# First layer's opening in a two-layer decoder trunk: row tiles abreast, norm weights and identity made on GpSimd, 13 unread products on TensorE

## The chip, the cores and the metric

One core of a Trainium2 chip runs the whole program. The metric is the device time of one execution in microseconds (us); lower is better. TensorE is PE in the profile (PEld its weight loads), VectorE is DVE, ScalarE is ACT, GpSimd is POOL, SyncE is SP. SP issues nearly all DMAs.

## The reference, cut to what matters

Two layers, each on 256 rows of 1024 (two row tiles of 128 rows), float32. The opening of a layer is a norm and an input projection; the rest of a layer (gated recurrence, compressed, selected and window attention, output projection, SwiGLU) is not touched.

```
for l in range(DEPTH):
    xn = rms_norm(h, norm_mix[l])            # x * rsqrt(mean(x*x) + 1e-6) * gain
    proj = xn @ w_in[l]                      # 1024 x 3352
    (hq, hf, hi, hg, nq, kc, vc, ksl, vsl, ksw, vsw, ngate) = split(proj)
    ...
    kc = compress(kc, pe_k, w1_k, w2_k); vc = compress(vc, pe_v, w1_v, w2_v)
    h = h + mix @ w_out[l]; h = h + ffn(rms_norm(h, norm_ffn[l]))
```

## The kernel before, in words

Every float32 product is made of three products of split halves: each weight tile (a "unit", up to 128x1024 float32) is loaded by SP into one of four buffers `wraw`, ACT copies it to a rounded high part `whi` (L142), DVE subtracts to a low part `wlo` (L143), and `mm3` (L319) issues high x high, low x high, high x low on PE. A raw buffer comes free when DVE has made `wlo`; there are six pairs of `whi`/`wlo`. `weights(i)` (L146) asks for splits AHEAD = 5 units ahead and loads NRAW = 4 further.

Units of a layer come in the order B (four units of 128x1024, the columns of kc, vc, ksl, vsl), C (four of 128x560: ksw, vsw, gates), A (four of 128x1024: the queries), then the recurrence's. I call them W0 to W3 (B), W4 to W7 (C), W8 to W11 (A).

The opening of layer 0: `norm_T` (L324) takes one row tile: ACT squares both halves with a row sum (L332), POOL makes the factor `n_ss` (L334, L335), DVE multiplies by factor and gain into `xn` (L338), PE transposes (`pxn`, L341), ACT copies the high part of the turned tile (L346), DVE subtracts the low part (L347). It is called for row tile 0 and then for row tile 1. The gain of the norm stands in one row; PE spreads it over 128 partitions with two products into PSUM (`pgain`, L249). The identity for transposes is loaded with the constants (L209). `setup_late` (L276) and `setup_tables` (L294) then make small vectors on DVE and rotary tables on POOL.

After B's products (`pt`, L322) ACT copies the first 256 columns of a row tile into `kvc` (L439), and PE transposes `kvc` into `pa` (L453). The compression's weights `w1` (L465: eight DMAs of 512 KB, k and v in turn, four steps) are multiplied in `phid` (L505) after A.

A scheduler of the framework puts the instructions of each engine into one fixed order before the run; each engine's sequencer, SP's too, works through its own row in order, and a wait holds up all that stands behind it. DMAs carry one of eight semaphores in turn; a DMA is issued only when the one eight before it has landed.

Of the kernel before, what the change touches and what calls it, by code (L numbers as in the profile page):

```python
# [23 lines left out]
EPS = 1e-6  # L24
# [65 lines left out]
def trunk(ctx: ExitStack, tc: tile.TileContext, x, w_in, w_out, lbl, gnorm, q_gain, k_gain,  # L90
          pe_k, w1_k, w2_k, pe_v, w1_v, w2_v, w_ffi, w_ffo, norm_mix, norm_ffn, consts, out):
    nc = tc.nc
# [11 lines left out]
    def bank(name, tag):  # L104
        return ps.tile([128, 512], F32, name=name, tag=tag, bufs=BANKS[tag])


    units = []

    def unit(src, a, b):  # L110
        units.append([src, a, b, None, None, None, None])
        return len(units) - 1

    state = {"loaded": 0, "split": 0}
# [11 lines left out]
    def after(ins, others):  # L126
        for o in others:
            tc.add_manual_dep(ins.ins, o.ins.name,
                              mybir.DependencyInfo(mybir.DependencyClass.NoSync, mybir.DependencyReason.DATA),
                              reason="fewer table loads")  # L130

    def split_to(n):
        while state["split"] < min(n, len(units)):
            load_to(state["split"] + 1)
            u = units[state["split"]]
            a, b = u[1], u[2]
            hi = wsp.tile([128, 1024], F32R, name="whi")
            lo = wsp.tile([128, 1024], F32R, name="wlo")
            u[4] = hi[:, : a * b].rearrange("p (a b) -> p a b", b=b)
            u[5] = lo[:, : a * b].rearrange("p (a b) -> p a b", b=b)  # L140
            with tc.high_priority(offset=SPLIT_PRIO):
                after(S.activation(u[4], u[3], AF.Copy), state.pop("behind", ()))  # L142
# [65 lines left out]
    cst = one.tile([128, NKEEP], F32, name="cst")  # L208
# [21 lines left out]
    def C(name, parts=128):  # L230
        lo, hi = _L[name]
        return cst[:parts, lo:hi]

    ident = C("ident")
    cos = C("cos").rearrange("p (t d) -> p t d", d=64)
    sin = C("sin").rearrange("p (t d) -> p t d", d=64)

# [6 lines left out]
    ones = one.tile([128, 128], F32, name="ones")
    nc.gpsimd.memset(ones[0:1], 1.0)
    gain0 = []
    for a in range(2):
# [6 lines left out]
    tabc = one.tile([128, NL, 2, 64], F32, name="tabc")  # L254

    kB = one.tile([128, 2, 2, T], F32R, name="kB")
    for g in range(2):
        nc.gpsimd.memset(kB[64 - 64 * g:128 - 64 * g, g].bitcast(F32), 0.0)

    def rstd(ss, n, div, name, scr=None):  # L260

# [14 lines left out]
    def setup_late():  # L276
        p = bank("prow", "c")
        PE.transpose(p[:, :NROW], rows[:NROW, :], ident[:NROW, :NROW])
        V.tensor_copy(vecs, p[:, :NROW])
        z = vecs[:, 0:8].rearrange("p (l h) -> p l h", h=4)  # L280
        mx = sm.tile([128, 4], F32, name="lbm")
        e = sm.tile([128, NL, 4], F32, name="lbe")
        sx = sm.tile([128, 4], F32, name="lbs")
        V.tensor_max(mx, z[:, 0], z[:, 1])
        V.tensor_sub(e, z, mx[:, None, :].to_broadcast([128, NL, 4]))
        S.activation(e, e, AF.Exp)
        V.tensor_add(sx, e[:, 0], e[:, 1])
        V.reciprocal(sx, sx)
        V.tensor_mul(e, e, sx[:, None, :].to_broadcast([128, NL, 4]))
        V.tensor_add(e[:, 1], e[:, 0], e[:, 1])  # L290
        V.tensor_sub(lb, e, e[:, 0:1].to_broadcast([128, NL, 4]))
        V.tensor_scalar(omlb, lb, -1.0, 1.0, op0=OP.mult, op1=OP.add)

    def setup_tables():  # L294
        G = nc.gpsimd
        V.tensor_copy(idb, ident)
        V.tensor_copy(cab, tmp0[:, :128])
        V.tensor_copy(lev_m, tmp0[:, 128:448])
        for l in range(NL):
            gq = qk_g[:, 64 * l:64 * l + 64]  # L300
            ks = [qk_g[:, NL * 64 + 192 * l + 64 * b:NL * 64 + 192 * l + 64 * b + 64] for b in range(3)]
            for i, g in enumerate((gq, ks[1], ks[2])):
                gb = g[:, None, :].to_broadcast([128, NT, 64])
                G.tensor_mul(tabs[:, l, i, 0], cos, gb)
                for a in range(2):
                    s0, s1 = slice(32 * a, 32 * a + 32), slice(32 - 32 * a, 64 - 32 * a)
                    G.tensor_mul(tabs[:, l, i, 1, :, s0], sin[:, :, s0],
                                 g[:, None, s1].to_broadcast([128, NT, 32]))
                if i == 0:
                    G.tensor_scalar(tabs[:, l, i], tabs[:, l, i], 0.125, None, op0=OP.mult)  # L310
            G.tensor_mul(tabc[:32, l, 0], C("cosc", 32), ks[0][:32])
            for a in range(2):
                s0, s1 = slice(32 * a, 32 * a + 32), slice(32 - 32 * a, 64 - 32 * a)
                G.tensor_mul(tabc[:32, l, 1, s0], C("sinc", 32)[:, s0], ks[0][:32, s1])


    products = []
# [6 lines left out]
    def norm_T(t, gain, xh, xl, tag, behind=(), hold=None):  # L324

        with tc.high_priority():
            ss = sm.tile([128, 4], F32, name="n_ss")
            lo = []
            xn = wk.tile([128, D], F32, name="xn", tag="vs", bufs=2)
            for a in range(2):  # L330
                cs = slice(512 * a, 512 * a + 512)
                sq = S.activation(xn[:, cs], h[:, t, cs], AF.Square, scale=D ** -0.5, accum_out=ss[:, a:a + 1])  # L332
                after(sq, behind)
# [22 lines left out]
    for l in range(NL):  # L356
        U = UN[l]
        gain1 = load_gain(norm_ffn[l])
        X = xT()
        last = [norm_T(0, gain0, *X[:2], "c", hold=end + HOLD[0] if l else None)[0]]  # L360
# [63 lines left out]
        def rope_k(src, b, t):  # L424
# [464 lines left out]
        X = X2  # L889
# [129 lines left out]
```

## Time and profile before

| | |
|---|---|
| median of 3 runs | 692.9 us (692.88 to 694.86) |
| the profiled execution's own time | 694.62 us |
| its span, first to last instruction | 692.2 us |
| PE busy | 674.9 us, 98% of the span |
| DVE, ACT, POOL busy | 477.8, 379.9, 23.1 us |
| DMA moved | 118.92 MB, mean 172 GB/s |

Time not in the span (694.62 - 692.2 = 2.4 us) lies around it. All starts are us from the span's start. A busy PE includes modelled ends of products, so starts are compared here, not lengths.

### The profile page before, as it was taken

What the parts mean: (1) busy time and instruction counts of PE and PEld (TensorE: products, weight loads), DVE (VectorE), ACT (ScalarE), POOL (GpSimd) and SP (SyncE); (2) the same over time, 40 slices, a digit from 0 to 9 for tenths busy, and PEclk for the clock granted to TensorE, in tenths of its full rate; (3) what the DMA queues carried; (4) which work ended last, traced back from release to release, by engine and by line L of the source; (5) the groups of instructions that cost most, each with busy time, mean ns of one, the idle gap of its engine ahead of it and who ended that gap; (6) DMA issues with size and microseconds to landing.
All of it is one profiled execution on the core that took longest, in us unless ns stands there. A gap on an engine that the chain in (4) does not pass through costs nothing.

```text
span 692.2 us, 10682 instructions
## 1 busy us (share of the span) xinstructions
PE 674.9 (98%) x4031; PEld 567.5 (82%) x4031; DVE 477.8 (69%) x853; ACT 379.9 (55%) x676; POOL 23.1 (3%) x54
## 2 busy tenths in 40 slices
PE   5999999999999999999999999999999999999997
PEld 3869886688988888888878898768898888888886
DVE  4879997586765566665678979958676655666552
ACT  5446766665555555555456557747545555555540
POOL 1700000001000000000010000000000000000000
PEclk9999999999999999999999999999999999999999
DMA  7798521253865566656678632404366665665521
GB/s 242 237 346 261 171 64 59 91 165 105 266 196 183 182 189 195 194 184 190 180 237 293 203 119 63 122 1 124 122 199 204 195 194 186 188 197 191 183 90 61
DMA packets 86568, 118.92 MB, mean 172 GB/s; under 512 B 5035, under 2 KB 69365, under 8 KB 86518
## 3 DMA queue, kind: packets, MB, share of 16 engines
q1 hardware_dynamic: 86518, 118.26, 55.2%
q8 instruction: 31, 0.51, 0.3%
q14 instruction: 19, 0.16, 0.1%
HBM read 117.19 MB, written 1.05 MB: 171 GB/s over the span
## 4 chain that ended last, share of the span: by engine, by line
PE 82%; DVE 7%; DMA 4%; ACT 4%; issue 2%; POOL 1%; SPq 0%; POOLq 0%; DVEq 0%; ACTq 0%
PE pgu L905 20%; PE pz L322 17%; PE pt L322 12%; PE pgu L908 10%; PE py L322 6%; DVE wlo L143 3%; DMA wraw<-in_w_in_dram 3%; PE pl L766 2%; PE pO L667 2%; ACT whi L142 2%; PE pPT L657 2%; PE pf L322 1%; PE pxn L341 1%; DMA wraw<-in_w_ffn_in_dram 1%; PE pq L322 1%
## 5 line engine op out<-in xcount | busy, mean ns | idle before, releaser
L143 DVE TENSOR_TENSOR wlo<-wraw,whi 128x1024 fp32r<-128x1024 f32 (+1 forms) x204 | 245.3, 1206 | 146.9 <-ACT whi L142 145.8
L142 ACT ACTIVATE whi<-wraw 128x1024 fp32r<-128x1024 f32 (+1 forms) x204 | 212.2, 1043 | 154.7 <-PE pgu L905 42.5
L905 PE MATMUL pgu<-x,whi 128*128 128x512 f32 x640 | 174.8, 394 | 0.1
L905 PEld LDWEIGHTS pgu<-x,whi 128*128 128x128 f32 x640 | 110.6, 189 | 16.0 <-DVE ahl L946 0.3
L322 PE MATMUL pz<-whi,ahl 128*128 128x512 f32 x352 | 112.5, 391 | 0.0
L908 PEld LDWEIGHTS pgu<-x,wlo 128*128 128x128 f32 x640 | 98.1, 189 | 13.5
L908 PE MATMUL pgu<-x,wlo 128*128 128x256 f32 x640 | 101.7, 281 | 0.0
L322 PE MATMUL pt<-whi,x 128*128 128x512 f32 (+1 forms) x320 | 100.0, 386 | 0.0
L322 PEld LDWEIGHTS pz<-whi,ahl 128*128 128x128 f32 x352 | 65.9, 188 | 13.9 <-DVE ahl L922 0.5
L322 PE MATMUL pz<-wlo,ahl 128*128 128x512 f32 x176 | 68.9, 392 | 0.0
L322 PEld LDWEIGHTS pt<-whi,x 128*128 128x128 f32 x320 | 57.5, 190 | 8.3 <-DVE x L347 0.5
L322 PE MATMUL pt<-wlo,x 128*128 128x512 f32 (+1 forms) x160 | 62.0, 388 | 0.6 <-DVE wlo L143 0.6
L322 PE MATMUL py<-whi,x 128*128 128x512 f32 x128 | 41.8, 397 | 0.0
L322 PEld LDWEIGHTS pz<-wlo,ahl 128*128 128x128 f32 x176 | 33.0, 188 | 6.4
L322 PEld LDWEIGHTS pt<-wlo,x 128*128 128x128 f32 x160 | 30.5, 191 | 5.3 <-DVE wlo L143 1.5
L587 ACT ACTIVATE P<-pS,nm 128x128 f32<-128x128 f32 (+1 forms) x64 | 26.0, 426 | 6.7 <-DVE nm L634 5.4
L322 PEld LDWEIGHTS py<-whi,x 128*128 128x128 f32 x128 | 24.1, 188 | 4.8
L914 ACT ACTIVATE sl<-sl 128x512 f32<-128x512 f32 x20 | 12.7, 633 | 27.3 <-DVE sl L913 27.3
L766 PEld LDWEIGHTS pl<-Q,K 128*128 128x128 f32 x160 | 23.7, 191 | 3.3 <-issue 0.8
L322 PE MATMUL py<-wlo,x 128*128 128x512 f32 x64 | 25.0, 390 | 0.0
L322 PE MATMUL pf<-x,whi 128*128 128x256 f32 x128 | 23.8, 286 | 0.0
L322 PE MATMUL pgt<-whi,x 128*128 128x256 f32 x128 | 23.8, 285 | 0.0
(220 smaller groups left out, 862.4 us busy)
## 6 DMA issues: line engine op xcount, KB each, us to landing
wraw<-in_w_ffn_in_dram SPq DMA_DIRECT2D x88, 512.0 KB, 3.6
wraw<-in_w_in_dram SPq DMA_DIRECT2D x48, 512.0 KB, 5.0
wraw<-in_w_ffn_out_dram SPq DMA_DIRECT2D x44, 512.0 KB, 3.5
w<-in_cmp_w_k_dram SPq DMA_DIRECT2D x8, 512.0 KB, 5.1
w<-in_cmp_w_v_dram SPq DMA_DIRECT2D x8, 512.0 KB, 7.3
wraw<-in_w_out_dram SPq DMA_DIRECT2D x16, 256.0 KB, 4.0
wraw<-in_w_out_dram SPq DMA_DIRECT2D x8, 512.0 KB, 3.9
wraw<-in_w_in_dram SPq DMA_DIRECT2D x8, 280.0 KB, 5.4
```

The lines of the kernel that those rows point to most:

```text
L142: after(S.activation(u[4], u[3], AF.Copy), state.pop("behind", ()))
L143: u[6] = V.tensor_sub(u[5], u[3], u[4].bitcast(F32))
L322: products.append(PE.matmul(o, a[u], b[v], start=start and i == 0, stop=stop and i == 2, skip_group_check=skip))
L341: tr = PE.transpose(p[:, 128 * k:128 * k + 128], xn[:, 512 * c + 128 * k:512 * c + 128 * k + 128], ident)
L587: e = S.activation(o, i, f, **kw)
L657: PE.transpose(p[:, 128 * hg:128 * hg + 128], P[t, g][:, hg, b, 128 * sb:128 * sb + 128], ident)
L667: m = PE.matmul(po[64 * g:64 * g + 64], vtok[:, b, sb, 64 * g:64 * g + 64], pts[g][0], start=(b == 0 and sb == 0), stop=False, skip_group_ ...
L766: m = PE.matmul(p[:, t0 + 64 * i:t0 + 64 * i + 64], K[:, i, ts], QF[:, i, ts].rearrange("p (n c a) -> p n c a", c=2, a=half)[:, :, 1], sta ...
L905: products.append(PE.matmul(pp[b], w[0][:, k, s], X[2][:, 4 * hh + k].rearrange("p c t -> p (c t)"), start=(hh == 0 and k == 0), stop=Fals ...
L908: products.append(PE.matmul(pp[b][:, T:], w[1][:, k, s], X[0][:, 4 * hh + k], start=False, stop=(hh == 1 and k == 3), skip_group_check=True))
L914: S.activation(sl, sl, AF.Silu)
```

## The change

It writes layer 0's opening as a routine of its own and moves small work about:

- `first_rows` replaces the two calls of `norm_T` in layer 0. It chains the instructions of ACT, DVE and POOL in a written order (tile 0's two halves, W0's split, tile 0's first half turned, tile 1's first half, W1's split, ...); the second halves are turned from inside the loop over B (`second`). `proj_first` walks B as (unit, row tile) = (0,0) (1,0) (0,1) (1,1) (2,0) (2,1) (3,0) (3,1) instead of all units of tile 0 and then of tile 1.
- POOL writes the identity (memset, affine_select) and spreads the gain row (two partition_broadcast of 512); the two products and the identity's DMA are gone. The gain row's DMA is issued by ACT.
- 13 products of a constant bfloat16 tile (128x512) into a bank that nobody reads stand first on PE.
- The zeroing of `kB` and the rotary tables are chained behind the factors on POOL, key tables ahead of query tables. `setup_late` moves behind B. Three casts (idb, cab, lev_m) move behind the split of W11.

```diff
-    DMA.dma_start(grow[0:1], norm_mix[0:1])
+    cst = one.tile([128, NKEEP], F32, name="cst")
+    S.dma_start(grow[0:1], norm_mix[0:1])
...
-    DMA.dma_start(cst[:, :128], consts[:, :128])
...
+    ident = one.tile([128, 128], F32, name="ident")
+    G.memset(ident, 1.0)
+    G.affine_select(ident, ident, pattern=[[-1, 128]], compare_op=OP.is_equal, fill=0.0, base=0, channel_multiplier=1)
+    grows = wk.tile([128, 2, 512], F32, name="grows", tag="P", bufs=1)
...
+        last_pool = G.partition_broadcast(grows[:, a], grow[0:1, 512 * a:512 * a + 512], channels=128)
...
-        gain0.append(bank("pgain", "b"))
-        PE.matmul(gain0[a], ones[0:1], grow[0:1, 512 * a:512 * a + 512], start=True, stop=True)
+    V.memset(idle, 1.0)
+    spin_bank = bank("pspin", "e")
+    def spin(n):
+        for _ in range(n):
+            PE.matmul(spin_bank, idle[:, :128], idle, start=True, stop=True)
+    spin(SPIN)
...
+        with tc.high_priority():
+            squares(0)
+            normed(0, 0)
+            normed(0, 1)
+            split()
+            pv = turned(0, 0)
+            hi(0, 0, pv)
+            lo(0, 0, pv)
+            squares(1)
+            normed(1, 0)
+            split()
+            pv = turned(1, 0)
+            hi(1, 0, pv)
+            lo(1, 0, pv)
+            normed(1, 1)
+        def second(t):
+            with tc.high_priority():
+                pv = turned(t, 1, products[-1:])
+                hi(t, 1, pv)
+                lo(t, 1, pv)
+                split()
...
-        if l == 0:
-            norm_T(1, gain0, *X[:2], "c", last)
-            setup_late()
+        if l:
+            norm_T(0, gain0, *X[:2], "c", hold=end + HOLD[0])
+        else:
+            second = first_rows(*X[:2])
             setup_tables()
...
+        def proj_first(name):
+            ps_ = [bank("pt", "a") for _ in range(NT)]
+            for q, t in ((0, 0), (1, 0), (0, 1), (1, 1), (2, 0), (2, 1), (3, 0), (3, 1)):
+                    w = weights(U[name, q]) if q > 1 and t == 0 else units[U[name, q]][4:6]
...
+                    if (q, t) in ((1, 0), (0, 1)):
+                        second(t)
...
+        if l == 0:
+            setup_late()
```

What the scheduler makes of it, at three places. First SP's DMA issues after the small constants; `gain` is the next norm's weights, `wraw` with 128x2x280 are C's units W4 to W7, `w_...<-in_cmp_w` with 128x4x256 are `w1`. Before:

```order
L200 DMA gain<-in_norm_ffn_dram 128x1024
L122 DMA wraw<-in_w_in_dram 128x2x280 x4
L465 DMA w_355<-in_cmp_w_k_dram 128x4x256
L122 DMA wraw<-in_w_in_dram 128x2x512 x4
L465 DMA w_355<-in_cmp_w_v_dram 128x4x256
L465 DMA w_358<-in_cmp_w_k_dram 128x4x256
```

The same place with the change, with what each issue waits for (a DMA semaphore, and POOL or DVE):

```order
L202 DMA gain<-in_norm_ffn_dram 128x1024 [waits DMAHW4_49,Pool_49]
L566 DMA w_367<-in_cmp_w_k_dram 128x4x256 [waits DMAHW5_49]
L566 DMA w_367<-in_cmp_w_v_dram 128x4x256 [waits DMAHW6_49]
L566 DMA w_370<-in_cmp_w_k_dram 128x4x256 [waits DMAHW7_49]
L566 DMA w_370<-in_cmp_w_v_dram 128x4x256 [waits DMAHW0_49]
L566 DMA w_373<-in_cmp_w_k_dram 128x4x256 [waits DMAHW1_49]
L123 DMA wraw<-in_w_in_dram 128x2x280 [waits DMAHW2_49,DVE_49]
L566 DMA w_373<-in_cmp_w_v_dram 128x4x256 [waits DMAHW3_49]
L566 DMA w_376<-in_cmp_w_k_dram 128x4x256 [waits DMAHW4_49]
L123 DMA wraw<-in_w_in_dram 128x2x280 [waits DMAHW5_49,DVE_49]
L566 DMA w_376<-in_cmp_w_v_dram 128x4x256 [waits DMAHW6_49]
L123 DMA wraw<-in_w_in_dram 128x2x280 [waits DMAHW7_49,DVE_49]
```

The fourth C unit is the next row after these. All eight `w1` loads now stand ahead of W7, five of them ahead of W4; before, the four C units stood ahead of all of them.

Second ACT's row around the end of B; 128x1024 and 128x560 `whi` are splits of B's and C's units. Before:

```order
L346 ACTIVATE x_128<-pxn 128x4x128 x2
L439 ACTIVATE kvc<-pt 128x512
L420 ACTIVATE sqk<-pt 128x128
L442 ACTIVATE vtok<-pt 128x128
L286 ACTIVATE lbe<-lbe 128x8
L142 ACTIVATE whi<-wraw 128x560 x3
L439 ACTIVATE kvc<-pt 128x512
L142 ACTIVATE whi<-wraw 128x560
```

With the change:

```order
L366 ACTIVATE x_141<-pxn 128x4x128
L143 ACTIVATE whi<-wraw 128x1024
L143 ACTIVATE whi<-wraw 128x560 x4
L538 ACTIVATE kvc<-pt 128x512
L505 ACTIVATE sqk<-pt 128x128
L541 ACTIVATE vtok<-pt 128x128
L538 ACTIVATE kvc<-pt 128x512
```

Both copies to `kvc` now stand behind the splits of all four C units, W7's among them; before, the first stood ahead of all of them and the second ahead of W7's.

Third PE's row from B's end on. Before (two rows of B's last products, then the rest):

```order
L322 MATMUL pt<-wlo,x_128 128x512
L322 MATMUL pt<-whi,x_128 128x512
L453 MATMUL pa<-cst,kvc 128x128 x2
L322 MATMUL pt<-whi,x_128 128x280
L322 MATMUL pt<-wlo,x_128 128x280
```

With the change, with waits:

```order
L528 MATMUL pt<-wlo,x_141 128x512 x2
L289 MATMUL prow<-ident,tmp_92 128x74 [waits DMAHW4_49,DMAHW3_49,DMAHW5_49,DMAHW2_49,PE_49]
L554 MATMUL pa<-ident,kvc 128x128 [waits Activation_49]
L554 MATMUL pa<-ident,kvc 128x128 [waits PE_49]
L335 MATMUL pt<-whi,x_141 128x280
L335 MATMUL pt<-wlo,x_141 128x280 [waits DVE_49]
```

In both, the first transposes of `kvc` stand ahead of C's first product.

## Rows read from the trace of the kernel before

**Rows 1.** The page: busy time of PE, its busy tenths in 40 slices.

```profile
PE 674.9 (98%) x4031; PEld 567.5 (82%) x4031; DVE 477.8 (69%) x853; ACT 379.9 (55%) x676; POOL 23.1 (3%) x54
...
PE   5999999999999999999999999999999999999997
```

**Rows 2.** Timeline of PE, opening (start us, us, what, count, idle before and its releaser).

```profile
11.83 1.97 PE L341 MATMUL pxn<-cst,xn 128*128 128x128 f32 x8 [5.78 <-DVE xn L338]
...
14.65 1.05 PE L322 MATMUL pt<-whi,x 128*128 128x512 f32 x2
15.51 0.53 PE L322 MATMUL pt<-wlo,x 128*128 128x512 f32 x1
15.88 0.63 PE L322 MATMUL pt<-whi,x 128*128 128x512 f32 x2
16.34 0.40 PE L322 MATMUL pt<-wlo,x 128*128 128x512 f32 x1
...
20.21 0.63 PE L341 MATMUL pxn<-cst,xn 128*128 128x128 f32 x4
...
27.16 0.38 PE L453 MATMUL pa<-cst,kvc 128*128 128x128 f32 x2
```

**Rows 3.** Timeline of ACT: the split of W0.

```profile
8.80 1.06 ACT L142 ACTIVATE whi<-wraw 128x1024 fp32r<-128x1024 f32 x1 [3.48 <-DMA wraw<-in_w_in_dram]
```

**Rows 4.** Timeline of POOL: the last memset, then the factor of row tile 0.

```profile
2.04 0.14 POOL L548 MEMSET kcz<- 128x64 f32 x1
...
5.42 0.29 POOL L334 TENSOR_SCALAR n_ss<-n_ss 128x1 f32<-128x1 f32 x1 [3.24 <-ACT xn L332]
5.80 0.57 POOL L335 TENSOR_TENSOR n_ss<-n_ss,mhalf 128x1 f32<-128x1 f32 x1
```

**Rows 5.** Timeline of DVE: normed halves, a unit's low part, a turned half's low part.

```profile
11.03 1.40 DVE L338 SCALAR_TENSOR_TENSOR xn<-h,n_ss,pgain 128x512 f32<-128x512 f32 x2
...
12.52 1.22 DVE L143 TENSOR_TENSOR wlo<-wraw,whi 128x1024 fp32r<-128x1024 f32 x1
...
13.66 0.68 DVE L347 TENSOR_TENSOR x<-pxn,x 128x512 fp32r<-128x512 f32 x1
```

**Rows 6.** Timeline of SP's queue: first issues, and those from the next norm's gain on.

```profile
0.72 0.36 SPq L205 DMA_DIRECT2D gain<-in_norm_mix_dram  x1
...
2.00 0.43 SPq L209 DMA_DIRECT2D cst<-in_consts_dram  x1
...
16.80 0.39 SPq L200 DMA_DIRECT2D gain<-in_norm_ffn_dram  x1
...
17.30 1.92 SPq L122 DMA_DIRECT2D wraw<-in_w_in_dram  x4
...
19.26 0.64 SPq L465 DMA_DIRECT2D w<-in_cmp_w_k_dram  x1
```

**Rows 7.** DMA issues in 16 to 50 us: KB each, median us to landing.

```profile
w<-in_cmp_w_k_dram SPq DMA_DIRECT2D x4, 512.0 KB, 8.0
...
wraw<-in_w_in_dram SPq DMA_DIRECT2D x4, 280.0 KB, 5.4
gain<-in_norm_ffn_dram SPq DMA_DIRECT2D x1, 512.0 KB, 4.7
```

**Rows 8.** Windows: busy us (count) of PE, PEld, DVE, ACT, POOL; clock, DMA share, GB/s.

```profile
21.00:25.00 4.00, 4.00 (x19) 3.30 (x18) 3.87 (x13) 3.30 (x8) 4.00 (x13) 1.00 1.06 354
26.00:29.00 3.00, 2.69 (x17) 2.21 (x16) 2.93 (x6) 1.49 (x4) 3.00 (x8) 1.00 0.02 3
...
40.00:50.00 10.00, 10.00 (x94) 7.18 (x93) 6.78 (x21) 2.03 (x3) 0.00 (x0) 1.00 1.10 348
```

**Rows 9.** Timeline of ACT around B's end: a copy to kvc, a split of 560.

```profile
27.36 0.60 ACT L439 ACTIVATE kvc<-pt 128x512 f32<-128x512 f32 x1 [2.57 <-PE pt L322]
27.86 0.66 ACT L142 ACTIVATE whi<-wraw 128x560 fp32r<-128x560 f32 x1
```

**Rows 10.** Waits of PE's weight loads in 26 to 90 us: total, times, longest.

```profile
PEld pt L322 <- DVE wlo L143: 1.5, 3, 0.8
```

More of the change, by code (lines that the diff above doesn't have):

```diff
@@ L43 @@
 LEV_PRIO, PACE = 250, (0, 7, 2)
+SPIN = 13
 HOLD, HOLD_C = (18, 18, 16, 36), 1
@@ L110, in unit @@
     def unit(src, a, b):
-        units.append([src, a, b, None, None, None, None])
+        units.append([src, a, b] + [None] * 5)
         return len(units) - 1
@@ L141, in split_to @@
             with tc.high_priority(offset=SPLIT_PRIO):
-                after(S.activation(u[4], u[3], AF.Copy), state.pop("behind", ()))
+                u[7] = S.activation(u[4], u[3], AF.Copy)
+                after(u[7], state.pop("behind", ()))
                 u[6] = V.tensor_sub(u[5], u[3], u[4].bitcast(F32))
@@ L232, in C @@
         return cst[:parts, lo:hi]
-    ident = C("ident")
+    G = nc.gpsimd
+    ident = one.tile([128, 128], F32, name="ident")
+    G.memset(ident, 1.0)
+    G.affine_select(ident, ident, pattern=[[-1, 128]], compare_op=OP.is_equal, fill=0.0, base=0, channel_multiplier=1)
+    grows = wk.tile([128, 2, 512], F32, name="grows", tag="P", bufs=1)
+    gain0 = []
+    for a in range(2):
+        last_pool = G.partition_broadcast(grows[:, a], grow[0:1, 512 * a:512 * a + 512], channels=128)
+        gain0.append(grows[:, a])
     cos = C("cos").rearrange("p (t d) -> p t d", d=64)
@@ L243, in trunk @@
     nc.gpsimd.memset(mhalf, -0.5)
[L244 to L247, printed above, removed]
-        gain0.append(bank("pgain", "b"))
-        PE.matmul(gain0[a], ones[0:1], grow[0:1, 512 * a:512 * a + 512], start=True, stop=True)
+    idle = one.tile([128, 512], BF16, name="idle")
+    V.memset(idle, 1.0)
[4 more added lines that the diff above has]
+    spin(SPIN)
     vecs = one.tile([128, NROW], F32, name="vecs")
@@ L256, in trunk @@
     kB = one.tile([128, 2, 2, T], F32R, name="kB")
-    for g in range(2):
-        nc.gpsimd.memset(kB[64 - 64 * g:128 - 64 * g, g].bitcast(F32), 0.0)
     def rstd(ss, n, div, name, scr=None):
@@ L294, in setup_tables, with then @@
     def setup_tables():
[L295 to L298, printed above, removed]
+        def then(ins):
+            after(ins, pool_order[-1:])
+            pool_order.append(ins)
+        for g in range(2):
+            then(G.memset(kB[64 - 64 * g:128 - 64 * g, g].bitcast(F32), 0.0))
         for l in range(NL):
@@ L301, in setup_tables @@
             ks = [qk_g[:, NL * 64 + 192 * l + 64 * b:NL * 64 + 192 * l + 64 * b + 64] for b in range(3)]
[L302 removed]
+            for i, g in ((1, ks[1]), (2, ks[2]), (0, gq)):
                 gb = g[:, None, :].to_broadcast([128, NT, 64])
[L304 removed]
+                then(G.tensor_mul(tabs[:, l, i, 0], cos, gb))
                 for a in range(2):
                     s0, s1 = slice(32 * a, 32 * a + 32), slice(32 - 32 * a, 64 - 32 * a)
[L307 to L308 removed]
+                    then(G.tensor_mul(tabs[:, l, i, 1, :, s0], sin[:, :, s0],
+                                      g[:, None, s1].to_broadcast([128, NT, 32])))
                 if i == 0:
[L310 to L311 removed]
+                    then(G.tensor_scalar(tabs[:, l, i], tabs[:, l, i], 0.125, None, op0=OP.mult))
+            then(G.tensor_mul(tabc[:32, l, 0], C("cosc", 32), ks[0][:32]))
             for a in range(2):
                 s0, s1 = slice(32 * a, 32 * a + 32), slice(32 - 32 * a, 64 - 32 * a)
[L314 removed]
+                then(G.tensor_mul(tabc[:32, l, 1, s0], C("sinc", 32)[:, s0], ks[0][:32, s1]))
     products = []
@@ L322, in mm3, with first_rows, then, split @@
             products.append(PE.matmul(o, a[u], b[v], start=start and i == 0, stop=stop and i == 2, skip_group_check=skip))
-    def norm_T(t, gain, xh, xl, tag, behind=(), hold=None):
+    pool_order = []
+    def first_rows(xh, xl):
+        xn, rs, order = [], [], {V: [], S: [], G: [last_pool]}
+        def then(eng, ins):
+            after(ins, order[eng][-1:])
+            order[eng].append(ins)
+        def split():
+            i = state["split"]
+            split_to(i + 1)
+            then(S, units[i][7])
+            then(V, units[i][6])
+        def normed(t, c):
+            cs = slice(512 * c, 512 * c + 512)
+            then(V, V.scalar_tensor_tensor(xn[t][:, cs], h[:, t, cs], rs[t], gain0[c], op0=OP.mult, op1=OP.mult))
+        def turned(t, c, behind=()):
+            p = bank("pxn", "c")
+            for k in range(4):
+                cs = slice(512 * c + 128 * k, 512 * c + 128 * k + 128)
+                after(PE.transpose(p[:, 128 * k:128 * k + 128], xn[t][:, cs], ident), behind)
+            return p.rearrange("p (k t) -> p k t", t=128)
+        def hi(t, c, pv):
+            dh = xh[:, 4 * c:4 * c + 4, 128 * t:128 * t + 128]
+            then(S, S.activation(dh, pv, AF.Copy))
+        def lo(t, c, pv):
+            sl = slice(4 * c, 4 * c + 4), slice(128 * t, 128 * t + 128)
+            then(V, V.tensor_sub(xl[:, sl[0], sl[1]], pv, xh[:, sl[0], sl[1]].bitcast(F32)))
+        def squares(t):
+            ss = sm.tile([128, 4], F32, name="n_ss")
+            xn.append(wk.tile([128, D], F32, name="xn", tag="vs", bufs=2))
+            for a in range(2):
+                cs = slice(512 * a, 512 * a + 512)
+                then(S, S.activation(xn[t][:, cs], h[:, t, cs], AF.Square, scale=D ** -0.5,
+                                     accum_out=ss[:, a:a + 1]))
+            then(G, G.tensor_scalar(ss[:, 2:3], ss[:, 0:1], ss[:, 1:2], EPS, op0=OP.add, op1=OP.add))
+            then(G, G.tensor_tensor(ss[:, 3:4], ss[:, 2:3], mhalf, op=OP.pow))
+            rs.append(ss[:, 3:4])
+        with tc.high_priority():
[19 more added lines that the diff above has]
+                split()
+        pool_order.extend(order[G])
+        return second
@@ L326, in norm_T @@
+    def norm_T(t, gain, xh, xl, tag, hold=None):
         with tc.high_priority():
@@ L331, in norm_T @@
                 cs = slice(512 * a, 512 * a + 512)
-                sq = S.activation(xn[:, cs], h[:, t, cs], AF.Square, scale=D ** -0.5, accum_out=ss[:, a:a + 1])
-                after(sq, behind)
+                S.activation(xn[:, cs], h[:, t, cs], AF.Square, scale=D ** -0.5, accum_out=ss[:, a:a + 1])
             nc.gpsimd.tensor_scalar(ss[:, 2:3], ss[:, 0:1], ss[:, 1:2], EPS, op0=OP.add, op1=OP.add)
@@ L433, in rope_k @@
             V.tensor_add(dst, dst, tmpk)
+        def proj_first(name):
+            ps_ = [bank("pt", "a") for _ in range(NT)]
+            for q, t in ((0, 0), (1, 0), (0, 1), (1, 1), (2, 0), (2, 1), (3, 0), (3, 1)):
+                    w = weights(U[name, q]) if q > 1 and t == 0 else units[U[name, q]][4:6]
+                    ts = slice(128 * t, 128 * t + 128)
+                    for i, (u, v) in enumerate(((0, 0), (1 - q % 2, q % 2), (q % 2, 1 - q % 2))):
+                        for k in range(2):
+                            products.append(PE.matmul(ps_[t], X[v][:, 2 * q + k, ts], w[u][:, k],
+                                                      start=(q + i + k == 0), stop=(q == 3 and i == 2 and k == 1)))
+                    if (q, t) in ((1, 0), (0, 1)):
+                        second(t)
+            return enumerate(ps_)
         begin = len(products)
-        for t, p in proj_tok("B"):
+        for t, p in proj_tok("B") if l else proj_first("B"):
             if l and t == 0:
@@ L494, in trunk @@
         gates(0)
+        if l == 0:
+            for o, i in ((idb, ident), (cab, tmp0[:, :128]), (lev_m, tmp0[:, 128:448])):
+                after(V.tensor_copy(o, i), [units[U["A", 3]][6]])
         p = bank("phid", "e")[:, :256]
```

2 lines of the change are left out of this document (removed).

## The prediction

> **What bounds the kernel now.** I read the page first: PE is busy for 674.9 us of the 692.2 us span, and its busy tenths are 9 in every slice but the first and the last [rows 1]. So the time is PE's work plus PE's holes, and PE's work does not change here (the 13 unread products run while PE has nothing else). Next I read PE's timeline. The first transposes start at 11.83, after an idle stretch of 5.78 us that DVE's `xn` ended; the first transposes of `kvc` (`pa`), which mark B's end, start at 27.16 [rows 2]. Up to there PE loses an opening; after it there are only small holes: its weight loads wait 1.5 us in all for `wlo` in `pt`, in three waits [rows 10]. Last I read what feeds PE after the opening. Products of B take 0.23 us from start to start, so PE eats a unit of 512 KB in 12 products, 2.8 us; the DMA engines are full wherever SP has issued (354 and 348 GB/s at a share of 1.06 and 1.10), and stand still in 26 to 29 us (3 GB/s), where SP itself waits [rows 8]. So two things can move the time: how early B ends, and when C's four units land relative to that.
>
> **The opening.** The change takes two issues ahead of W0 off SP's row, 0.36 and 0.43 us [rows 6], so all later landings of the opening come about 0.8 us earlier: W0, which ACT took at 8.80 [rows 3], lands at 8.0. The factor of tile 0 is ready at 6.37 before [rows 4], but DVE's fixed order held `xn` back to 11.03 behind W0's low part; now `xn` stands ahead of it. From W0's low part on (8.0 + 1.06 for `whi` = 9.1) DVE still has four low parts of units at 1.22, four of turned halves at 0.68 and two normed halves at 0.70 [rows 5]: 9.0 us, so W3's low part is there at 18.1 at the earliest. The last unit's 12 products after it take 2.8 us, which makes 20.9; hand-offs between ACT, PE and DVE (tile 1's factor, two rounds of transposes) cost 0 to 3 us. B ends between 21 and 24 instead of at 27.16: a lead of 3 to 6 us at that point.
>
> That leaves out what POOL's new work costs ahead of the factor, for which no row has a price: two code loads (they show as the custom rows of POOL's order), an affine_select, two partition_broadcasts. From below it is nothing, since POOL waited 3.24 us for ACT between its last memset and the factor [rows 4]. From above, that same stretch held one code load before, so a load costs at most 3.2 us by it. If POOL makes the factor late by d, B's end moves by at most d. I shall show that d up to about 13 us changes nothing. The 13 products cost nothing for the same reason; so do the moved casts, the zeroing of `kB` and the identity.
>
> **What gives the lead back.** The order of SP decides. Before, C's four units were issued right behind the gain row of the next norm, in one stretch from 17.30 to 19.22, and the first `w1` load behind them at 19.26 [rows 6]. Now all eight `w1` loads stand ahead of W7, and five ahead of W4. They need no buffer that anyone holds, so nothing delays them into the right place; their data is wanted only in `phid`, after A. In the trace of before the data move in the order of issue: 280 KB units land in 5.4 us while `w1` loads behind the backlog take 8.0 [rows 7].
>
> When W7 lands: the gain row was issued at 16.80 and took 4.7 us [rows 6, 7]; 0.8 us earlier that is a landing at 20.7. Behind it lie 8 x 512 KB and 4 x 280 KB = 5.34 MB. At 348 to 354 GB/s [rows 8] they take 15.2 us, and with eight loads allowed in flight the queue does not run dry. **W7 lands at 35.9.** On ACT both copies to `kvc` now stand behind the splits of all four C units, W7's last. So the first copy ends 0.66 + 0.60 us later [rows 9], at 37.2, and PE's `pa`, which waits for it and has all of C behind it, starts at 37.2 instead of 27.16: **+10.0 us**. PE stands idle for some 14 us from B's end. Since that end (21 to 24) lies 13 us ahead of 37.2, the opening's whole gain is worth nothing, and POOL's unknown price costs nothing up to there.
>
> **The clock.** Before 15.88 products of 512 columns start 0.43 us apart (14.65 to 15.51 for two), after it 0.23 (15.88 to 16.34) [rows 2]: 1.2 GHz against 2.4 GHz, although the granted clock reads 1.00 in all windows. The slow stretch followed an idle one of 5.78 us. It cost eight transposes about 0.09 each (1.97/8 against 0.63/4) and five products 0.20 each: 1.7 us. After 14 us of idling I expect the same again: +1.7; the bounds are 0 and 1.7. The Trainium skill (TensorE: Matmul & The Clock Gate, Part 1) says that the throttled state is the default and that activity releases it; by that rule the price is paid after this hole too, and the sum stands at +10.2, without it at +8.5. No idle stretch after the opening is long enough in this trace to show it.
>
> **After the hole** all `w1` and C weights are there, and DVE has nothing left over from B. I take the three waits for `wlo` as gone: -1.5 [rows 10]. W8 to W11 follow W7 directly, with their buffers freed as C's low parts are made; PE has C's 6 us ahead of them. Two more table loads of ACT and `setup_late` fall into this stretch, where ACT is not what PE waits for.
>
> **Sum:** +10.0 + 1.7 - 1.5 = +10.2 us. Against the profiled execution's 694.6 us that is 704.8. That execution lies 1.7 us above the median of the three runs; on the median of 692.9 the forecast is **703.1 us**.
>
> **The rivals.**
> A, faster: the C weights do not come late, and the opening's lead stays. It would need DMAs to overtake one another, or B to end no earlier than C's weights arrive anyway. Then PE's `pa` starts at about 23, 4 us earlier: 692.9 - 4 = 688.9. It decides if W7 is there by 22. For it: B's chain on DVE does get shorter by the rows above. Against it: 4.2 MB of `w1` stand in front in SP's order, 12 us of transfer at the measured rate, and the landings of before follow the issues. Chance 0.07.
> B, slower still: POOL becomes the bound. SP's gain row now waits for the broadcasts, and everything behind it in SP's order moves one for one once they end after 16.0. From 2.2 us [rows 4] two loads at the bound of 3.2 us leave over 7 us for the select and the broadcasts, so it takes a broadcast of more than 3 us each. If they end at 20, the time is 707. Chance 0.10. The Trainium skill (GPSIMD Engine Reference, 2.1 Instruction dispatch) gives about 6 us for the first call of a freshly loaded kernel. By that, an estimate, the loads alone end at about 14, the broadcasts at 16 to 18, and the time is 703 to 705; the row's 3.24 us speaks against 6 for the load that before had, and none here shows one that swaps libraries.
> C, the hole is partly made up: with every weight on hand PE runs without the small holes that before had up to 90 us, the clock stays up, and the stretch ends 2 to 6 us later only: 695 to 699. Chance 0.08, of which 0.03 lie within 0.3%.
>
> **How the numbers follow.** The forecast has 0.75. Its own range: W7 lands 1 us earlier or later (5% of the rate), the clock costs 0 to 1.7, the waits after the hole come out between -3 and +2. That is +6.0 to +14.7, or 698.9 to 707.6. C's upper part and B's lower part lie in or beside it; I take 698.0 to 707.6, which leaves out A and the outer parts of B and C. 0.3% (2 us) is about what a measurement can tell from no change. Faster 0.07 (A), within it 0.03 (part of C), slower 0.90.
>
> **What would show it.** PE: first transposes at 7 to 9, if POOL is quick; the last B product at 21 to 24; then a hole to 36 to 38, ended by ACT's `kvc`, whose own idle time is ended by the DMA of `wraw`. SP: five `w1` issues between the gain row and W4. DMA: no still stretch at 26 to 29. Products right after the hole 0.43 us apart. The split of W7 at 36. I am wrong if `pa` starts before 33, if C's units land ahead of `w1`, or if the factor of tile 0 comes later than 22.

## The result, and the profile after

The changed kernel takes **702.77 us** (median of 4 runs, 701.65 to 703.84), the kernel before 693.02 us (4 runs beside it): a ratio of 1.0134, 95% interval 1.0111 to 1.0158, or +9.75 us by the medians and +9.3 by the ratio. The forecast was 703.1 us in a range of 698.0 to 707.6. The two profiled executions lie at opposite ends of their runs (the one before at the top, with 694.6 us; this one at the bottom, with 701.65 and a span of 699.6), so they differ by 7.4 us of span, not by 9.75.

The page of the changed kernel, against [rows 1]: PE's busy time and its busy tenths.

```profile
PE 674.7 (96%) x4040; PEld 568.4 (81%) x4040; DVE 475.6 (68%) x854; ACT 383.7 (55%) x678; POOL 28.3 (4%) x57
...
PE   3799999999999999999999999999999999999997
```

PE's busy time is the same within 0.2 us (674.9 before). What differs is the first two slices of 17.5 us, in which PE is busy for 3 and 7 tenths; from the third on PE is full, as before.

PE's timeline (start us, us, what, count, idle before and its releaser), against [rows 2]:

```profile
1.50 5.31 PE L260 MATMUL pspin<-idle 128*128 128x512 bf16 x13 [1.50 <-DVE idle L255]
20.58 1.12 PE L361 MATMUL pxn<-ident,xn 128*128 128x128 f32 x4 [13.77 <-DVE xn L355]
22.38 1.22 PE L528 MATMUL pt<-whi,x 128*128 128x512 f32 x2 [0.69 <-ACT x L366]
23.40 1.05 PE L528 MATMUL pt<-wlo,x 128*128 128x512 f32 x2
...
36.37 0.62 PE L528 MATMUL pt<-wlo,x 128*128 128x512 f32 x2
36.83 0.23 PE L289 MATMUL prow<-ident,tmp 74*128 74x74 f32 x1
37.52 0.44 PE L554 MATMUL pa<-ident,kvc 128*128 128x128 f32 x2 [0.46 <-ACT kvc L538]
```

The marks are the first transposes at 20.58 (11.83 before) and `pa` at 37.52 (27.16 before): +8.75 and +10.36 us. The hole is 13.77 us long, as long as the forecast had it, but it stands **ahead** of B and was ended by DVE's `xn`. At B's end only 0.46 us are idle. So the size came out, and the place did not.

What DVE waited for is on POOL, against [rows 4] (the second figure is the length in us, the bracket the idle time before):

```profile
1.41 0.29 POOL L238 TENSOR_SCALAR_AFFINE_SELECT ident<-ident 128x128 f32<-128x128 f32 x1 [0.30 <-issue]
9.91 1.48 POOL L242 PARTITION_BROADCAST grows<-gain  x2 [8.22 <-issue]
18.75 0.31 POOL L379 TENSOR_SCALAR n_ss<-n_ss 128x1 f32<-128x1 f32 x1 [7.36 <-issue]
19.14 0.60 POOL L380 TENSOR_TENSOR n_ss<-n_ss,mhalf 128x1 f32<-128x1 f32 x1
```

"issue" means that the profile shows nothing that POOL waited for. These are 8.22 us ahead of the first broadcast, and 7.36 us ahead of `n_ss`. The inputs of `n_ss` were there: ACT's sums of tile 0 ended at 5.87. The landing of the gain row, which the broadcasts read, is not in this trace; issued at the same 0.78, it released PE at 2.29 in e8 and at 3.18 in e10 (experiments below), so up to 1.5 of the 8.22 us may be a wait for it. In POOL's order a code load stands at each of these two places, and one more ahead of the select, where only 0.30 us are idle; e1 below, which has neither broadcast, has neither long stretch. The factor of tile 0 is ready at 19.74 instead of 6.37, 13.4 us late. The two broadcasts themselves take 0.74 us each, the select 0.29.

The forecast's other mark held as well: W7's split on ACT starts at 36.30, and is followed by the first `kvc`.

```profile
36.30 0.67 ACT L143 ACTIVATE whi<-wraw 128x560 fp32r<-128x560 f32 x1 [0.47 <-DMA wraw<-in_w_in_dram]
36.88 0.58 ACT L538 ACTIVATE kvc<-pt 128x512 f32<-128x512 f32 x1
```

From these rows alone both stories fit: B ended late because of POOL, and C's last unit came late as forecast. The order of SP was as forecast too (`w` are the `w1` loads, `wraw` the units):

```profile
15.61 0.39 SPq L202 DMA_DIRECT2D gain<-in_norm_ffn_dram  x1
...
18.41 2.64 SPq L566 DMA_DIRECT2D w<-in_cmp_w_k_dram  x1
22.35 0.37 SPq L123 DMA_DIRECT2D wraw<-in_w_in_dram  x1
...
26.55 0.37 SPq L123 DMA_DIRECT2D wraw<-in_w_in_dram  x1
...
31.45 6.76 SPq L123 DMA_DIRECT2D wraw<-in_w_in_dram  x6
```

But look at when the units are issued. The fifth `w1` issue ended at 21.05, and W4 goes out at 22.35, after SP has waited for 1.3 us. DVE's timeline has the reason:

```profile
19.77 1.41 DVE L355 SCALAR_TENSOR_TENSOR xn<-h,n_ss,grows 128x512 f32<-128x512 f32 x2 [18.33 <-POOL n_ss L380]
21.11 1.22 DVE L145 TENSOR_TENSOR wlo<-wraw,whi 128x1024 fp32r<-128x1024 f32 x1
...
25.30 1.22 DVE L145 TENSOR_TENSOR wlo<-wraw,whi 128x1024 fp32r<-128x1024 f32 x1
...
29.93 1.49 DVE L145 TENSOR_TENSOR wlo<-wraw,whi 128x1024 fp32r<-128x1024 f32 x1 [0.26 <-ACT whi L143]
```

W0's low part ends at 21.11 + 1.22 = 22.33, W1's at 26.52, W2's at 31.42; W4, W5 and W6 are issued at 22.35, 26.55 and 31.45, and W7 at 33.2, behind W3's low part. The four units of C go into the four buffers of B, and each is issued as soon as the low part of its predecessor frees one. SP's own waits between 14 and 40 us (total us, times, longest) say the same:

```profile
SPq L123 <- DVE wlo L145: 10.4, 7, 3.9
```

So in this execution it was not the 4.2 MB of `w1` ahead of them that made C late, but POOL again, by way of the buffers. The forecast's 35.9 for W7 was met by another mechanism. Whether the order of SP would have done it too is what the experiments had to show.

### The profile page after: what moved, and what is told of

Same layout as the page of the kernel before. It is cut to its first block, busy times and chain, and to the rows that moved or that the text cites. A ratio compares the mean times of both kernels' runs of the same rounds, so it can differ in the third digit from the quotient of the medians.

```text
span 699.6 us, 10719 instructions
## 1 busy us (share of the span) xinstructions
PE 674.7 (96%) x4040; PEld 568.4 (81%) x4040; DVE 475.6 (68%) x854; ACT 383.7 (55%) x678; POOL 28.3 (4%) x57
## 4 chain that ended last, share of the span: by engine, by line
PE 83%; DVE 5%; DMA 3%; POOL 3%; ACT 3%; issue 1%; SPq 1%; POOLq 0%; DVEq 0%; ACTq 0%
PE pgu L1009 21%; PE pz L335 17%; PE pgu L1012 11%; PE pt L335 9%; PE py L335 6%; PE pf L335 3%; DVE wlo L145 2%; PE pl L870 2%; PE pgt L335 2%; PE pPT L761 2%; PE pq L335 2%; PE pO L771 2%; DMA tmp<-in_consts_dram 1%; DMA w<-in_cmp_w_k_dram 1%; PE phid L609 1%
## 5 line engine op out<-in xcount | busy, mean ns | idle before, releaser
L143 ACT ACTIVATE whi<-wraw 128x1024 fp32r<-128x1024 f32 (+1 forms) x204 | 212.1, 1043 | 153.6 <-PE pgu L1009 43.9
L335 PE MATMUL pt<-whi,x 128*128 128x512 f32 (+1 forms) x288 | 91.2, 385 | 0.0
L335 PEld LDWEIGHTS pt<-whi,x 128*128 128x128 f32 x288 | 51.5, 189 | 6.3 <-DVE x L432 0.2
L335 PE MATMUL pt<-wlo,x 128*128 128x512 f32 (+1 forms) x144 | 55.1, 382 | 0.0
L335 PEld LDWEIGHTS pt<-wlo,x 128*128 128x128 f32 x144 | 27.2, 189 | 2.9
L870 PEld LDWEIGHTS pl<-Q,K 128*128 128x128 f32 x160 | 25.6, 191 | 3.9 <-PE pt L335 0.4
L870 PE MATMUL pl<-Q,K 128*128 128x64 f32 x160 | 24.1, 257 | 0.0
```

The source lines that it names most:

```text
L143: u[7] = S.activation(u[4], u[3], AF.Copy)
L870: m = PE.matmul(p[:, t0 + 64 * i:t0 + 64 * i + 64], K[:, i, ts], QF[:, i, ts].rearrange("p (n c a) -> p n c a", c=2, a=half)[:, :, 1], sta ...
```

## The experiments

Two suspects, each of which may be enough: POOL's two code loads, and SP's order. The first four kernels take away one, the other, and both, and put the order alone into the kernel before. All ratios are against the kernel before, on the same chip.

**Both suspects gone (e1).** The gain is spread by PE as before, the identity is still POOL's:

```diff
-    last_pool = G.partition_broadcast(grows[:, a], grow[0:1, ...], channels=128)
+    PE.matmul(gain0[a], ones[0:1], grow[0:1, ...], start=True, stop=True)
```

The gain's two products stand between the first eight and the last five of the 13 unread ones. With the broadcasts gone the scheduler puts C's units ahead of all `w1` loads again, as in the kernel before; so SP's order in the change was its answer to the broadcasts.

> The changed kernel, but PE spreads the norm gain by two products as before, so POOL has no broadcast and swaps no code; without it SP's row comes out with C's four units ahead of the w1 loads again. Both suspects are gone at once. Theory POOL (the two swaps of 8.2 and 7.4 us made the 10 us, C's late weights cost nothing beside them) and theory twins (swaps and order each put pa at about 37 by itself) both expect B to end at 21 to 24, pa at 22 to 25, and 688 to 691 us. If it stays above 697, a third cause is at work: the new order of the row tiles itself.

Measured: 696.01 us, ratio 1.0022 (1.0002 to 1.0042). Nearly 8 of the 9.3 us are gone, but the kernel is not faster than before: the time lies above the range of both theories and just below the 697 that was named for a third cause. PE's timeline:

```profile
8.24 0.60 PE L363 MATMUL pxn<-ident,xn 128*128 128x128 f32 x4
...
23.44 0.38 PE L556 MATMUL pa<-ident,kvc 128*128 128x128 f32 x2
...
35.53 0.50 PE L337 MATMUL pt<-wlo,x 128*128 128x512 f32 x1 [1.72 <-DVE wlo L145]
```

B does end where the forecast had it without POOL (21 to 24): `pa` at 23.44, 3.7 us ahead of the kernel before. Then PE waits 2.1 us for low parts of A. So there was a third cause, below; it is not the order of the row tiles, which the expectation named.

**POOL's loads alone (e2).** The changed kernel with every `w1` load of layer 0 behind the fourth C unit:

```diff
+    after(ld, loads[7:8])    # ld: a w1 load; loads[7]: the load of W7
```

> The changed kernel with the broadcasts and their swaps, but every w1 load of layer 0 stands behind the fourth C unit on SP; the rest as the change has it. Theory order (C's late weights made the 10 us, as predicted): W7 lands at about 24, and 690 to 694 us. Theories POOL and twins: B ends at 36 to 37 all the same, pa at 37 to 38, and 700 to 703 us, at most 1.5 us below the change.

Measured: 703.71 us, 1.0119 (1.0087 to 1.0151). No faster than the change. SP's timeline, then ACT's:

```profile
21.45 17.00 SPq L124 DMA_DIRECT2D wraw<-in_w_in_dram  x8
```

```profile
36.37 0.67 ACT L144 ACTIVATE whi<-wraw 128x560 fp32r<-128x560 f32 x1 [1.68 <-DMA wraw<-in_w_in_dram]
36.95 0.58 ACT L539 ACTIVATE kvc<-pt 128x512 f32<-128x512 f32 x1
```

With no `w1` load ahead of them the units still waited for their buffers: eight `wraw` issues (C's and A's) spread over 17 us from 21.45 on, and W7's split came at 36.37, as in the change (36.30). "W7 lands at about 24" was wrong under every theory, because I had not counted the buffers. `pa` came at 37.58. POOL's loads alone are worth the whole loss, as far as it can be measured.

**SP's order alone, in the changed kernel (e3).** No loads on POOL; the `w1` loads are emitted ahead of B's products and the loads of W4 to W6 held behind them; `kvc` is held behind W7's split, and `phid` behind A, where the change has them.

```diff
+    load_w1()
+    early.update({4: w1d[4:5], 5: w1d[6:7], 6: w1d[7:8]})
...
+    after(cp, [units[U["C", 3]][7]])
```

> No swaps on POOL (gain spread by PE, as in the kernel without loads), but the eight w1 loads forced ahead of C's four units on SP, both kvc copies behind W7's split on ACT, phid behind A on PE. Theories order and twins: B ends at 21 to 24, W7 lands at 35 to 36.5, pa at 36 to 38 after a hole of 12 us or more, and 699 to 704 us. Theory POOL: DMAs or PE make it up, and 688 to 693 us.

Measured: 702.45 us, 1.0103 (1.0073 to 1.0133). PE's timeline, then ACT's:

```profile
23.12 0.23 PE L298 MATMUL prow<-ident,tmp 74*128 74x74 f32 x1
33.69 0.83 PE L344 MATMUL pt<-whi,x 128*128 128x280 f32 x2 [10.34 <-ACT whi L150]
...
36.96 0.63 PE L581 MATMUL pa<-ident,kvc 128*128 128x128 f32 x2
```

```profile
32.96 0.67 ACT L150 ACTIVATE whi<-wraw 128x560 fp32r<-128x560 f32 x1 [7.35 <-DMA wraw<-in_w_in_dram]
...
34.67 1.43 ACT L150 ACTIVATE whi<-wraw 128x560 fp32r<-128x560 f32 x2 [0.21 <-DMA wraw<-in_w_in_dram]
```

This is the forecast's picture: B ends at 23.35, a hole of 10.3 us, the splits of C between 32.96 and 36.1 as their loads land. `pa` stands behind a part of C here and starts at 36.96. Without a swap on POOL the time is that of the change (702.77, measured on another occasion) within 0.3 us by the medians; by the ratios it is 2.2 us less (1.0103 against 1.0134), with intervals that overlap.

**SP's order alone, in the kernel before (e4).** The same hold on the loads, nothing else of the change.

> The kernel before with one thing changed: the eight w1 loads stand ahead of C's four units on SP (phid is held behind A's products, as it stood). B ends at 27 as before. Theories order and twins: C's products wait for W7, which lands at 36 to 37.5, C ends about 7 to 9 us later than before, and 699 to 702 us. Theory POOL: at most 3 us more, 692 to 696 us.

Measured: 701.38 us, 1.0095 (1.0065 to 1.0124). B ends at 27.6, and C's first product waits for its split (PE's timeline):

```profile
27.64 0.38 PE L476 MATMUL pa<-cst,kvc 128*128 128x128 f32 x2
...
35.38 0.84 PE L329 MATMUL pt<-whi,x 128*128 128x280 f32 x2 [6.02 <-ACT whi L149]
```

**What follows.** By the ratios, times 694 us, order alone costs 6.6 and 7.2 us (e4, e3), POOL's loads alone 8.3 (e2), both together 9.3, with intervals that overlap. The kernels e2, e3 and the change carry the rest of the change as well; counted from e1, which has neither suspect, the costs are 6.7 (e2), 5.6 (e3) and 7.8 us (the change). The two lie beside each other in time: either makes C's end late, and taking away only one gives back 1.0 (e2) or 2.2 us (e3) by the ratios, inside the intervals. A study that removed one suspect would have acquitted it.

**The third cause.** In e1 DVE stood still before A's first low part (DVE's timeline):

```profile
29.81 0.65 DVE L562 TENSOR_TENSOR flat<-pa,vecs 64x480 f32<-64x480 f32 x1 [2.07 <-POOL flat L550]
...
30.66 1.21 DVE L145 TENSOR_TENSOR wlo<-wraw,whi 128x1024 fp32r<-128x1024 f32 x1
```

It waited 2.07 us for POOL's zeroing of `flat`, which now stands behind all the table work in POOL's fixed order (POOL's timeline):

```profile
28.84 0.94 POOL L550 MEMSET flat<- 128x1024 f32 x1
```

Behind it on DVE stood the low parts of A. Two repairs were tried: `flat` zeroed between the factors of the two row tiles, and on top of it the Exp of the gate floors ahead of both sigmoids, which takes two table loads off ACT.

```diff
+    after(nc.gpsimd.memset(flat, 0.0), [last_pool])          # e5, ahead of first_rows
+    after(S.activation(gate[:, t], ..., AF.Sigmoid), [state["exp"]])   # e6, with e5's
```

> The kernel without loads (e1), and POOL zeroes flat between the factors of the two row tiles instead of behind all the table work. In e1 pa stood at 23.44, 3.7 us ahead of the kernel before, yet the time was 2 us above it; DVE waited 2.07 us for this zeroing, and PE then 2.1 us for low parts of A. Theory flat: the wait of DVE goes, A's waits for wlo fall to under 0.5, and 692 to 694.5 us. Theory DVE (from 30 to 90 us DVE is full in every kernel, so a lead is eaten whatever stands first): PE waits for other low parts instead, and 695 to 697.5 us.

> As e5, and ACT's Exp of the gate floors stands ahead of both sigmoids of gate instead of between them, which takes two table loads of 1.28 us off ACT's row. Theory tables: the splits of W9 to W11 come up to 2.6 us earlier, and with flat early the lead of 3.7 us at pa is kept in large part: 690 to 692.5 us. Theory flat alone: like e5, 692 to 694.5. Theory DVE: 695 to 697.5 us.

Measured: e5 692.99 us, 0.9981 (0.9962 to 1.0000); e6 695.33 us, 1.0018 (0.9996 to 1.0041). In e5 POOL zeroes `flat` at 6.12 and is done at 7.07 (POOL's timeline):

```profile
6.12 0.95 POOL L451 MEMSET flat<- 128x1024 f32 x1
```

That is worth 3.0 us against e1 by the medians (2.8 by the ratios; e1 and e5 ran on two chips), and the stretch from `pa` to the first product of the feed-forward part shrinks by about the same: 153.6 us (23.53 to 177.15) against 156.7 in e1 (23.44 to 180.13). "Theory flat" stands by the time, and with it a lead at `pa` is kept, which "theory DVE" denied; its other sign missed, since PE still waits 1.0 us for a low part of A (2.1 in e1), and not under 0.5. No gain from the table loads is shown: e6 is above e5, and of the same pair without the products (e8 and e10, below) the one with the Exp ahead is 0.8 us the slower, with intervals that overlap. The median of e6 lies in the range that "theory DVE" gave; that of e8, which is e6 without the products, does not, so what e6 lost is not DVE's. Why e6's runs reach from 693.2 to 698.5 is the next point.

**The 13 products.** The profiled execution of e6 is the slowest of its runs (698.5). PE's timeline:

```profile
1.50 3.60 PE L258 MATMUL pspin<-idle 128*128 128x512 bf16 x8 [1.50 <-DVE idle L253]
5.03 3.78 PE L263 MATMUL pgain<-gain,ones 1*128 1x512 f32 x4
8.74 2.31 PE L258 MATMUL pspin<-idle 128*128 128x512 bf16 x5
10.85 1.06 PE L363 MATMUL pxn<-ident,xn 128*128 128x128 f32 x4
```

and the chain that ended last, of the first 30 us (start us, us, what):

```profile
1.50 3.60 PE pspin L258 x8
5.10 3.71 PE pgain L263 x4
8.81 2.25 PE pspin L258 x5
```

The unread products stood on the chain, ahead of the first transposes: all 13 are 0.43 to 0.46 us apart, and the gain's products take 3.78 us. In the profiled execution of e5, with the same instructions on PE up to there, the last five products are 0.25 apart and the gain's take 2.27 us, and the transposes start at 8.32 instead of 10.85 (PE's timeline of e5):

```profile
7.23 1.25 PE L258 MATMUL pspin<-idle 128*128 128x512 bf16 x5
8.32 0.60 PE L363 MATMUL pxn<-ident,xn 128*128 128x128 f32 x4
```

PE came to the full rate by about 7 us there and at about 17 here; the granted clock of the windows reads 1.00 in both. So two kernels without the products were set against their twins, one of which was run again beside it:

> As e6 without the 13 unread products. Theory warm (they spare PE a slow start once nothing else makes the opening late): the first products of B start 0.43 us apart, pa 1 to 2.5 us later than in e6, and 0 to 2 us more than e6. Theory nothing (the two gain products do the same): pa within 0.5 us of e6 and the same time within 0.7 us.

> As e5 (no swaps, flat zeroed early) without the 13 unread products; the pair e6 and e8 differed in the same way and in nothing else. There the profiled run with products kept PE at 0.43 us per product until 17 us and had pa at 28.1, the one without at 23.1. Theory products hurt (they stand ahead of the first transposes on PE, and when PE stays at the slow rate they make the opening late): 691 to 693.5 us, highest run under 695, 0 to 2 us less than e5 beside it. Theory products help: 1 us or more above e5. Both below the kernel before by 0.5 to 3 us.

> The kernel of e5 once more, beside e10 on one chip: its runs lay between 691.7 and 695.5, in two groups. Theory products hurt: again two groups, the upper 2 to 4 us above the lower, median 692.5 to 694.5. Theory products help: one group, median below e10.

Measured: e8 692.97 us, 0.9979 (0.9962 to 0.9995), 2.4 us under e6; e10 **692.17 us**, 0.9967 (0.9953 to 0.9981); e11 693.44 us, 0.9991 (0.9977 to 1.0004). The highest run without products is 694.3 (e8) and 694.1 (e10), with them 698.5 (e6) and 695.5 (e5). "Theory products hurt" stands by the times. The runs of e11 fall in two groups again, seven at 691.9 to 693.8 and five at 695.0 to 695.4. Neither theory of e8 had its result: `pa` stands at 23.10, 5.0 us ahead of e6's 28.06. Where the upper group loses its time is seen in one execution only, that of e6. The profiled executions of e5 and e11 are of the lower group, and their `pa` (23.53 and 23.07) lies where it lies without products (23.10 in e8, 23.96 in e10), although B's first products are 0.43 us apart or more in e8 and e10 too, until about 12 and 14. In e10 PE starts with the gain's products, and its first transposes wait 0.21 us (PE's timeline):

```profile
3.18 3.75 PE L263 MATMUL pgain<-gain,ones 1*128 1x512 f32 x4 [3.18 <-DMA gain<-in_norm_mix_dram]
7.14 1.11 PE L363 MATMUL pxn<-ident,xn 128*128 128x128 f32 x4 [0.21 <-DVE xn L357]
...
23.96 0.38 PE L559 MATMUL pa<-ident,kvc 128*128 128x128 f32 x2
```

e10 is the fastest version here, 2.2 us below the kernel before beside it, and by the ratios (0.9967 and 1.0134) 11.6 us below the change. It keeps the change's order of the row tiles and its identity from POOL, and drops the broadcasts, the products and the late zeroing of `flat`.

**Can products hold the clock where POOL is late?** As e2, with 68 of them (e9).

> The changed kernel with C ahead of w1 (e2), and 68 unread products instead of 13, enough to run until the first transposes at 19.7. In e2 the granted clock fell to 0.50 in 10 to 25 us. Theory clock: granted clock 1.00 throughout, B's first products 0.23 us apart, pa at 36 to 36.6 instead of 37.58, and 0.8 to 1.8 us less than e2. Theory DVE: B is paced by DVE's low parts at 1.22 each, not by PE's clock, so pa and the time stay within 0.5 us of e2.

Measured: 703.86 us, 1.0149 (1.0100 to 1.0199); e2 had 703.71. PE's timeline, and windows (columns as in [rows 8]):

```profile
1.51 16.16 PE L261 MATMUL pspin<-idle 128*128 128x512 bf16 x67 [1.51 <-DVE idle L256]
21.22 1.11 PE L362 MATMUL pxn<-ident,xn 128*128 128x128 f32 x4 [3.55 <-DVE xn L356]
```

```profile
13.00:16.00 3.00, 2.95 (x15) 1.35 (x15) 0.00 (x0) 0.00 (x0) 0.00 (x0) 1.00 0.34 108
...
22.00:25.00 3.00, 2.31 (x7) 1.60 (x6) 1.65 (x2) 2.63 (x6) 0.64 (x2) 0.50 0.28 65
```

The granted clock was held at 1.00 to the end of the products, as expected; but in this execution, the slowest of the four (708.86 us), POOL's loads took 8.06 and 8.15 us, 1.5 us more than in e2, the transposes came 3.55 us after the last product, and the clock was at 0.50 (1.2 GHz) when B began. So the case that was to be tested did not occur, and what the clock is worth there stays open; the time did not move.

## Why the prediction was right, and where it was not

**The sum** was +10.2 us, and +9.75 was measured. The forecast had 0.75 and its mechanism, C's units behind `w1`, is real: it alone costs 6.6 to 7.2 us (e4, e3). But it did not set the time of the changed kernel, and the sum was met by luck: a second cost of about the same size stood in its place. Nor does the profiled pair add up to +10.2. There the terms are +10.36 at `pa` and -3.0 from there to the end of the span, 7.4 in all; the other 2.3 us of the 9.75 are differences between executions of the two kernels, and no trace here shows what makes them.

**The failed step is POOL's price.** "A load costs at most 3.2 us by it" took a row in which one load and a wait for ACT overlapped [rows 4] as a bound for all loads. Measured: 8.22 and 7.36 us in the change, 5.90 and 8.78 in e2, 8.06 and 8.15 in e9 (the first of each pair, ahead of the broadcasts, may hold up to 1.5 us of waiting for the gain row). The load in [rows 4] is the first of its program. In the change the first load, ahead of the select, shows 0.30 us of idling, and in e1 none; so that row priced a first load, and it bounds nothing for a swap in mid-stream. The Trainium skill (GPSIMD Engine Reference, 2.1 Instruction dispatch) has about 6 us for a freshly loaded kernel: the nearer figure, and still low for five of these six; and the swap back costs as much as the swap out. By rival B two loads at 6 us would have given 703 to 705. Rival B's own mechanism, SP's gain row behind the broadcasts, did not happen: these ended at 11.4 and the row went out at 15.61, ahead of the 16.0 from which it would have cost time.

**"d up to about 13 us changes nothing"** is right in time (d was 13.4, and e3 without these loads lies 0.3 us from the change by the medians, 2.2 by the ratios) and wrong in its reason. I held W7's landing to be independent of d. It hangs on d through the four buffers: the later B's low parts, the later C's issues. That I missed although the sentence "they need no buffer that anyone holds" was written for `w1` in the same paragraph; for C the opposite holds.

**B's end at 21 to 24** was right for an opening without loads (23.4 in e1, 23.35 in e3); in the change it was 36.99. **W7 at 35.9**: its split started at 36.30; with the order as the only cause its split started by 35.4 in e3, so the transfer sum (5.34 MB at 348 to 354 GB/s) was good to about a microsecond. SP's order and the missing still stretch of the DMA engines were as forecast.

**The clock.** Forecast: +1.7 after the hole. The granted clock fell in the hole, which stood elsewhere (windows, columns as in [rows 8]):

```profile
10.00:13.00 3.00, 0.00 (x0) 0.00 (x0) 0.00 (x0) 0.00 (x0) 1.39 (x2) 0.50 0.96 359
...
22.00:25.00 3.00, 2.62 (x6) 2.13 (x7) 1.38 (x3) 2.50 (x6) 1.21 (x3) 0.50 1.10 357
```

0.50 from 10 to 25 us, 1.2 of 2.4 GHz, after the unread products had ended at 6.81; the first products of B are again 0.43 to 0.51 us apart (22.38 to 24.26 for four). After `pa` two products of C take 0.25 us (39.32 to 39.57). In e3, where the hole does stand at B's end, they take 0.47 (34.86 to 35.33), so the price that I put behind the hole is there when the hole is. From the first transposes to `prow` it took 16.25 us, against 15.14 in e1, where PE's same order ran at the full rate from the start of B: 1.1 us, ahead of `pa` and not behind it. What B's end would have been at the full rate no run shows, since e9 did not get there. The Trainium skill (TensorE: Matmul & The Clock Gate, Part 1) calls the throttled state the default and has activity release it; these rows agree with it, while the start of e6, with PE at work from 1.50 and its products slow until about 17, shows the release only then.

**After the hole** I took 1.5 us off for small waits. From `pa` to the first feed-forward product it is 150.0 us in the change (37.52 to 187.55) and 152.5 before (27.16 to 179.64): 2.5 off, and 2.7 in e3 (36.96 to 186.72). This is what rival C named, at 2 to 3 us rather than 4 to 8.

**"The 13 products cost nothing"** held because POOL hid them: they ended at 6.81, and the first transposes came at 20.58. In an opening that is not held up they cost 0.8 to 2.4 us by the medians (e5 and e10, on two chips, by 0.8; e11 and e10 by 1.3; e6 and e8 by 2.4), with five of them behind the gain's products; all 13 at the front, as the change has them, were not tried there. The zeroing of `flat`, which I passed over as moved POOL work, costs 3 us as soon as the lead is there to be lost.

**Rival A**, a lead of 4 us and 688.9, was too high: with the loads, SP's order, `flat` and the products all dealt with, the lead at `pa` is 3.2 us and the time 2.2 us below before.

## What to carry to other kernels

Where a change makes two things late at once, undo both before you judge either: here each alone cost 6.6 to 8.3 us, both together 9.3, and repairing one showed nothing clear of the noise. Count, for every transfer that a sum assumes to start on time, whose buffer it goes into and what frees it; the queue's order is only one of the two gates. And a new kind of instruction on POOL in a hot opening is priced by its code loads, out and back, not by the 0.3 to 0.7 us that it runs.

## What the runs showed of the hardware

A code load on POOL in mid-stream went with 5.90 to 8.78 us of idling, six times in three kernels. The three swaps back ahead of the factor, whose inputs had long been there, took 7.36, 8.78 and 8.15 us; the three ahead of the broadcasts (8.22, 5.90, 8.06) may hold up to 1.5 us of waiting for the gain row. The first load, ahead of the affine_select at the start, shows 0.30 us of idling in the change and none in e1, and e1, which has only that one, shows no swap back.

PE's rate at the start of a run is not settled by keeping it busy: with the same instructions from 1.50 us on, products came from 0.43 to 0.23 us apart by about 7 us in one execution (e5) and at about 17 in another (e6), while the granted clock of the windows reads 1.00 throughout both. The profile's clock column does not show this slow rate; the spacing of the products does.
